# Selections, state-space products and gate products tied to the newest matmul, and engine orders from a time-line model

## The chip, the cores and the metric

The kernel runs on one core of one Trainium2 chip, as one launch. The metric is the device time in microseconds (us), the median of several runs. A core has a matrix engine (TensorE, PE in the profile; its weight loads are PEld), VectorE (DVE), ScalarE (ACT), GpSimd (POOL) and SyncE (SP), each with an instruction queue of its own that is worked off in order, and queues of DMA transfers that SP, ACT and POOL start. Matmuls write into PSUM, of which the kernel uses eight banks by turns; everything else lies in SBUF.

## What is computed

Two transformer-like blocks over 512 tokens of width 1024, all in float32. The first is a feed-forward layer, attention of several kinds (compressed, selected, windowed) and a second feed-forward layer. The second is a gated linear recurrence beside a state-space layer (the mix), and then a layer of 16384 small experts (PEER). The parts that the change touches, cut:

```python
def _s5(u, a_re, a_im, log_dt, b_re, b_im, c_re, c_im, d_skip, w_glu, b_glu):
    ...
    bb_re = coef_re * br - coef_im * bi
    bb_im = coef_re * bi + coef_im * br
    ...
    _, _, xr, xi = lax.associative_scan(combine, (a_re_t, a_im_t, bu_re, bu_im), axis=1)
    ...

def _peer(h, w_q, keys1, keys2, u_tab, v_tab):
    ...
    def block(hb):
        qh = (hb @ w_q).reshape(tb, PEER_HEADS, 2, PEER_HALF)
        s1 = jnp.einsum('thd,nd->thn', qh[:, :, 0], keys1)
        s2 = jnp.einsum('thd,nd->thn', qh[:, :, 1], keys2)
        v1, i1 = lax.top_k(s1, PEER_TOPK)
        v2, i2 = lax.top_k(s2, PEER_TOPK)
        cand = (v1[..., :, None] + v2[..., None, :]).reshape(tb, PEER_HEADS, kk)
        cidx = (i1[..., :, None] * PEER_NKEYS + i2[..., None, :]).reshape(tb, PEER_HEADS, kk)
        best, pos = lax.top_k(cand, PEER_TOPK)
        eidx = jnp.take_along_axis(cidx, pos, axis=-1)
        gates = jax.nn.softmax(best.astype(jnp.float32), axis=-1).astype(hb.dtype)
        act = jax.nn.gelu(jnp.einsum('td,thkd->thk', hb, u_tab[eidx]), approximate=False)
        return jnp.einsum('thk,thkd->td', gates * act, v_tab[eidx])
```

## The kernel before

**Products.** A large product is written as three matmuls on split operands (`mm3`: high and low part of the weights and of the input), 512 columns each. `weight` loads a 128 x 1024 block by SP (`raw`), casts it on ScalarE (`whi`, L173) and subtracts on VectorE, in one stage on GpSimd, to get the low part (`wlo`, L174); it does so two blocks ahead of their use. A product of one such block is 24 matmuls.

**Order of the program.** `weave` writes the program. A main generator gives the large products; side generators give the rest. `self.clk` adds up a rough time of all matmuls written so far (model time, in ns), and a side that yields 8000 goes on when 8000 of it have passed. So every side instruction has a place among the matmuls. That place is not binding: when the program is complete, the framework lays out the queue of each engine by running the instructions through a model of the machine. There an instruction may go ahead of those written before it on its engine once all that it depends on is done, so one that depends on nothing late can be laid out long before its place. Then waits between engines are set by the data and buffers alone.

**Preparation of the state space** (`s5_prepare`): a side of the second feed-forward stage. For each of four quarters it makes two groups of six elementwise instructions of 512 or 576 columns on GpSimd, by the helpers `mul`, `sub` and `add` (L1015 to L1021), then transposes, stores to HBM and some VectorE work.

**Routing of the experts** (`peer_route`): while the products of the experts run, VectorE finds the sixteen best candidates per token and head. `select(t, gap)` turns them, for 128 tokens (tile t of 4), into numbers of experts and gates: a subtraction on GpSimd (L1522), Exp on ScalarE (L1523), and twice a conversion (L1538, L1539), sixteen comparisons `eq` (L1548) and two sums `sel` (L1553) on VectorE; four transposes bring the result into `routeT` and `routeG`. `dense(t)` then makes a dense table of gates out of it: for each token a one-hot matrix `a` (GpSimd, L1569) and `b` (VectorE, L1570), one matmul (`b,a`), and two instructions that put the result into `stage` (ScalarE L1594, VectorE L1595), which goes to HBM. The one-hots are made two groups of four tokens ahead. `select(0)` is written ahead of `dense(0)`, `select(t + 1)` beside `dense(t)`, in thirteen steps of 8000 of model time.

**Experts' second half** (`peer`, `load`): for each of 128 blocks of experts the activations come back from HBM (`t`), are multiplied by the gates on GpSimd (L1687) and split on ScalarE (`pwh`, L590) and VectorE (`pwl`, L591). Sixteen groups of eight blocks; each group's are loaded while the group before is multiplied.

Of the kernel before, what the change touches and what calls it, by code (L numbers as in the profile page):

```python
# [13 lines left out]
ALU = mybir.AluOpType  # L14
AX = mybir.AxisListType
# [7 lines left out]
FT = 22  # L23
GB = 16
AHEAD = 2


class Weights:
# [21 lines left out]
class Prog:  # L50
# [23 lines left out]
    def mm(self, out, lhsT, rhs, start, stop):  # L74
        n = m = 1
        for x in rhs.shape[1:]:
            n *= x
        for x in lhsT.shape[1:]:
            m *= x
        p = 4 if lhsT.dtype == F32 else 1  # L80
        self.clk += max(n * 0.4217 * p, m * 0.84 * (2 if p == 4 else 1))
        self.nc.tensor.matmul(out, lhsT=lhsT, rhs=rhs, start=start, stop=stop)  # L82

    def tr(self, out, x, ident):
        self.clk += 54
# [132 lines left out]
    def small(self, n, w=4):  # L218
        t = self.big.tile([128, 64], F32, tag="rs_small", bufs=3, name=self.name("rs"))
        return [t[:, w * i:w * i + w] for i in range(n)]  # L220
# [791 lines left out]
        return pn  # L1012

    def mul(self, eng, out, a, b):
        eng.tensor_tensor(out, a, b, op=ALU.mult)  # L1015

    def sub(self, eng, out, a, b):
        eng.tensor_tensor(out, a, b, op=ALU.subtract)

    def add(self, eng, out, a, b):  # L1020
        eng.tensor_tensor(out, a, b, op=ALU.add)  # L1021

    def mix_consts(self):
        nc, A, ph = self.nc, self.A, self.ph
# [13 lines left out]
    def s5_prepare(self):  # L1038
        nc, A, ph = self.nc, self.A, self.ph
# [87 lines left out]
        for j in range(4):  # L1127
# [4 lines left out]
            pr, pi = (pd[:, i, :, q].rearrange("p l g -> p g l")[:, :, :, None].to_broadcast(sh) for i in range(2))  # L1132
            br, bi = (bb[:, i, q, :][:, :, None, :].to_broadcast(sh) for i in range(2))
            t, R = self.t2k(), [self.t2k(), self.t2k()]
            self.mul(g, f4(R[0]), pr, br)
            self.mul(g, f4(t), pi, bi)
            self.sub(g, R[0], R[0], t)
            self.mul(g, f4(R[1]), pr, bi)
            self.mul(g, f4(t), pi, br)
            self.add(g, R[1], R[1], t)  # L1140
            yield 13000
            for i in range(2):
                ps = self.ps()
                for a in range(4):
# [8 lines left out]
            cr, ci = (m["s5c"][:, i, q, :][:, :, None, :].to_broadcast(sh) for i in range(2))  # L1153
            ca = [ph.tile(sh, F32, tag="ca", bufs=3, name=self.name("ca")) for _ in range(3)]
            flat = lambda t: t.rearrange("p g l h -> p (g l h)")
            self.mul(g, ca[0], pr, cr)
            self.mul(g, ca[2], pi, ci)
            self.sub(g, flat(ca[0]), flat(ca[0]), flat(ca[2]))
            self.mul(g, ca[1], pnb, cr)
            self.mul(g, ca[2], pr, ci)  # L1160
            self.sub(g, flat(ca[1]), flat(ca[1]), flat(ca[2]))
            yield 15000
            for i in range(2):
                g.dma_start(second[:, 1024 + 576 * i:1600 + 576 * i], flat(ca[i]))
            ps = self.ps()
# [304 lines left out]
    def peer_route(self, st, box):  # L1470
# [46 lines left out]
        TG = ph.tile([128, 512, 2], F32, name="routeG")  # L1517

        def select(t, gap):
            gate = small(128, F32, "gate", 2)  # L1520
            gv = gate.rearrange("p (h k) -> p h k", h=8)
            g.tensor_tensor(gv, best[:, t], best[:, t, :, 0:1].to_broadcast([128, 8, 16]), op=ALU.subtract)  # L1522
            nc.scalar.activation(gate, gate, AF.Exp)  # L1523
            sm = small(8, F32, "gsum", 2)
            v.tensor_reduce(sm, gv, axis=AX.X, op=ALU.add)
            v.reciprocal(sm, sm)
            v.tensor_tensor(gv, gv, sm[:, :, None].to_broadcast([128, 8, 16]), op=ALU.mult)
            gh = small(128, F32R, "gateh", 2)
            gl = small(128, F32, "gatel", 2)
            v.tensor_copy(gh, gate)  # L1530
            v.tensor_tensor(gl, gate, gh.bitcast(F32), op=ALU.subtract)
            yield gap
            sel = []
            p2 = pos[:, t].rearrange("p h k -> p (h k)")
            for i, (op, c) in enumerate(((ALU.logical_shift_right, 4), (ALU.bitwise_and, 15))):
                ji = small(128, U32, "ji", 2)
                jf = small(128, F32, "jf", 2)
                v.tensor_scalar(ji, p2, c, None, op0=op)  # L1538
                v.tensor_copy(jf, ji)  # L1539
                o = small(128, F32, "sel", 4)  # L1540
                xf = ph.tile([128, 8, 16], F32, tag="idxf", bufs=2, name=self.name("xf"))
                v.tensor_copy(xf, idx[i][:, t])
                eq = ph.tile([128, 128, 16], F32, tag="eq", bufs=1, name=self.name("eq"))

                ev = eq.rearrange("p (h k) j -> p h k j", h=8)
                jv = jf.rearrange("p (h k) -> p h k", h=8)
                for j in range(16):
                    v.scalar_tensor_tensor(ev[:, :, :, j], jv, float(j), xf[:, :, j:j + 1].to_broadcast([128, 8, 16]),  # L1548
                                           op0=ALU.is_equal, op1=ALU.mult)
                    if j % 4 == 3:  # L1550
                        yield gap
                for s in (slice(0, 64), slice(64, 128)):
                    v.tensor_reduce(o[:, s], eq[:, s], axis=AX.X, op=ALU.add)  # L1553
                    yield gap
                sel.append(o)
            ps = self.ps()
            for i, x in enumerate(sel + [gh.bitcast(F32), gl]):
                self.tr(ps[:, i * 128:(i + 1) * 128], x, self.ident)
            ts = slice(t * 128, (t + 1) * 128)
            for i in range(2):  # L1560
                nc.scalar.copy(T2[i][:, ts], ps[:, i * 128:(i + 1) * 128])
            nc.scalar.copy(TG[:, ts, :].rearrange("p t x -> p x t"), ps[:, 256:512].rearrange("p (x t) -> p x t", x=2))
# [12 lines left out]
        def dense(tile):  # L1575
            t1 = tile * 128
            ab = [onehots(t1), onehots(t1 + 4)]
            yield 5500
            due = self.clk
            for t0 in range(0, 128, 4):  # L1580
                if t0 % GB == 0:
                    stage = ph.tile([128, 128, GB], F32, tag="stage", bufs=3, name=self.name("stage"))
                a, b = ab.pop(0)
                pss = [self.ps(), self.ps()]
                for i in range(4):
                    self.mm(pss[i // 2][:, (i % 2) * 256:(i % 2) * 256 + 256], lhsT=a[:, i, :],
                            rhs=b[:, i].rearrange("p x e -> p (x e)"), start=True, stop=True)
                if t0 + 8 < 128:
                    ab.append(onehots(t1 + t0 + 8))
                for i in range(2):  # L1590
                    o = t0 % GB + 2 * i
                    sv = stage[:, :, o:o + 2].rearrange("p e t -> p t e")
                    pv = pss[i].rearrange("p (t x e) -> p t x e", t=2, x=2)
                    nc.scalar.copy(sv, pv[:, :, 0])  # L1594
                    v.tensor_tensor(sv, sv, pv[:, :, 1], op=ALU.add)  # L1595
                if t0 % GB == GB - 4:
                    nc.scalar.dma_start(self.gd[(t1 + t0) // GB], stage)
                due = max(due + self.pace, self.clk - 3000)
                yield max(0, due - self.clk)
# [29 lines left out]
    def peer(self, st, done):  # L1629
# [53 lines left out]
        def load(e):  # L1683
            t = self.t2k()
            nc.scalar.dma_start(t, gs[e])
            yield 3600
            g.tensor_tensor(f(t), f(t), gts[e // 8][:, :, e % 8, :], op=ALU.mult)  # L1687
            yield 2600
            hi = self.ph.tile([128, 512], F32R, tag="pwh", bufs=16, name=self.name("pwh"))
            lo = self.ph.tile([128, 512], F32R, tag="pwl", bufs=16, name=self.name("pwl"))  # L1690
# [249 lines left out]
```

## Time and profile before

| what | us |
|---|---|
| median of three runs | 3064.87 |
| lowest and highest | 3063.09, 3072.38 |
| the profiled execution | 3067.61 |
| its span, first to last instruction | 3065.8 |
| TensorE busy in it | 3001.5 (98%) |
| VectorE, ScalarE, GpSimd busy | 2052.5, 1167.6, 1068.7 |

The stages follow one another: first feed-forward to about 405 us, attention to 760, second feed-forward to 1190, mix to 1475, candidates for the experts to 1715, dense gates to 2284, the second half of the experts to the end. TensorE is close to full everywhere, so the profile is read by its gaps: who released it, and what that engine did before. A row of a time line gives start and duration in us, the engine and line, what it writes and reads, how many equal instructions follow each other (x8), and in brackets the idle time of its engine before it, with the releaser.

### The profile page before, as it was taken

The page shows a single profiled execution, that of the slowest core. Times are in us where ns is not written, and L with a number is a line of the kernel's source. Part 1 is how long each engine was busy: PE and PEld are TensorE (multiplying, and loading weights), DVE is VectorE, ACT ScalarE, POOL GpSimd, SP SyncE. Part 2 cuts the span into 40 slices and gives each one's busy share as a digit, 9 for nine tenths or more (in the row PEclk, how much of TensorE's full clock was granted, in tenths as well). Part 3 has the DMA queues.
Part 4 walks back from the last instruction along what each step waited for, and adds up shares of the span by engine and source line. Part 5 has one row for each costly group of instructions (what it writes and reads, how often), then busy time and mean ns, then how long its engine had stood idle before and what let it go on. Part 6 is the DMA issues. An engine that isn't in the chain of part 4 may idle for free.

```text
span 3065.8 us, 40068 instructions
## 1 busy us (share of the span) xinstructions
PE 3001.5 (98%) x14672; PEld 2470.7 (81%) x14672; DVE 2052.5 (67%) x3902; ACT 1167.6 (38%) x1851; POOL 1068.7 (35%) x1016
## 2 busy tenths in 40 slices
PE   8999999999999999899999899999999999999998
PEld 6888886667887889787888788888887888888887
DVE  7455457775768656874778998878863655665653
ACT  4222334453422236444433354545443322332232
POOL 1000110002344422012345787878752423322321
PEclk9999999999999999999999999999999999999999
DMA  6344322113535443222333355555557656656642
GB/s 200 105 146 137 96 87 83 49 39 95 169 116 182 158 135 118 77 71 83 99 111 120 130 194 191 189 188 192 183 197 248 219 189 208 192 183 194 201 138 76
DMA packets 140324, 443.54 MB, mean 145 GB/s; under 512 B 16720, under 2 KB 19568, under 8 KB 135008
## 3 DMA queue, kind: packets, MB, share of 16 engines
q1 hardware_dynamic: 82512, 285.41, 29.4%
q10 hardware_dynamic: 42624, 101.73, 9.1%
q0 software_dynamic: 14992, 53.85, 5.6%
q8 instruction: 116, 1.90, 0.3%
q14 instruction: 80, 0.66, 0.1%
HBM read 361.88 MB, written 77.86 MB: 143 GB/s over the span
## 4 chain that ended last, share of the span: by engine, by line
PE 71%; DVE 5%; DMA 1%; issue 1%; ACT 1%; POOL 1%; DVEq 0%; ACTq 0%; POOLq 0%
PE ps L82 70%; DVE wlo L174 1%; DVE eq L1548 1%; DMA t<-act_d 1%; PE ps L86 1%; POOL t L823 0%; DVE sel L1553 0%; POOL t L1687 0%; ACT whi L173 0%; DMA act_d<-t 0%; DVE h L1817 0%; ACT t L966 0%; DVE jf L1539 0%; DVE t L821 0%; DVE t L591 0%
## 5 line engine op out<-in xcount | busy, mean ns | idle before, releaser
L173 ACT CAST whi<-raw 128x1024 fp32r<-128x1024 f32 (+2 forms) x505 | 516.7, 1025 | 1114.0 <-PE ps L82 886.9
L82 PE MATMUL ps<-xhi,whi 128*128 128x512 f32 (+1 forms) x2232 | 873.7, 392 | 12.3 <-ACT whi L173 10.8
L82 PE MATMUL ps<-xhi,wlo 128*128 128x512 f32 (+1 forms) x2232 | 862.1, 387 | 2.7 <-POOL wlo L174 1.8
L82 PE MATMUL ps<-xlo,whi 128*128 128x512 f32 (+1 forms) x2232 | 862.7, 387 | 0.8 <-DVE xlo L382 0.7
L174 DVE TENSOR_TENSOR wlo<-raw,whi 128x1024 fp32r<-128x1024 f32 (+2 forms) x469 | 603.6, 1287 | 136.7 <-ACT whi L173 126.1
L82 PEld LDWEIGHTS ps<-xhi,whi 128*128 128x128 f32 x2232 | 421.2, 189 | 105.3 <-issue 14.1
L1569 POOL TENSOR_SCALAR a<-iota,routeT 128x128 fp32r<-128x128 f32 x512 | 459.8, 914 | 108.0 <-PE ps L82 107.9
L82 PEld LDWEIGHTS ps<-xhi,wlo 128*128 128x128 f32 x2232 | 420.3, 189 | 91.3 <-POOL wlo L174 2.2
L82 PEld LDWEIGHTS ps<-xlo,whi 128*128 128x128 f32 x2232 | 420.7, 189 | 80.3 <-issue 2.5
L82 PE MATMUL ps<-pwh,whi 128*128 128x512 f32 (+1 forms) x1048 | 403.3, 385 | 1.5 <-ACT pwh L590 1.5
L82 PE MATMUL ps<-pwh,wlo 128*128 128x512 f32 (+1 forms) x1048 | 403.2, 385 | 1.1 <-DVE wlo L174 1.1
L82 PE MATMUL ps<-pwl,whi 128*128 128x512 f32 (+1 forms) x1048 | 403.4, 385 | 0.3 <-DVE pwl L591 0.2
L1687 POOL TENSOR_TENSOR t<-t,gt 128x512 f32<-128x512 f32 x128 | 199.2, 1576 | 421.1 <-DMA t<-act_d 367.0
L1570 DVE SCALAR_TENSOR_TENSOR b<-iota,routeT,routeG 128x256 fp32r<-128x256 f32 x512 | 232.2, 503 | 64.5 <-PE ps L82 64.5
L1823 DVE SCALAR_TENSOR_TENSOR h<-ps,mod,h 128x512 f32<-128x512 f32 (+1 forms) x131 | 96.4, 736 | 220.5 <-PE ps L82 220.5
L82 PEld LDWEIGHTS ps<-pwh,whi 128*128 128x128 f32 x1048 | 197.1, 188 | 41.0 <-ACT pwh L590 2.1
L82 PEld LDWEIGHTS ps<-pwh,wlo 128*128 128x128 f32 x1048 | 197.4, 188 | 40.5 <-DVE wlo L174 1.5
L82 PEld LDWEIGHTS ps<-pwl,whi 128*128 128x128 f32 x1048 | 197.3, 188 | 40.1 <-DVE pwl L591 1.0
L1594 ACT COPY stage<-ps 128x256 f32<-128x256 f32 x256 | 137.8, 643 | 162.0 <-PE ps L82 152.8
L591 DVE TENSOR_TENSOR pwl<-t,pwh 128x512 fp32r<-128x512 f32 x128 | 140.7, 1127 | 45.4 <-ACT pwh L590 40.8
L268 POOL TENSOR_TENSOR acc<-acc,sq 128x512 f32<-128x512 f32 x18 | 32.0, 1777 | 382.2 <-ACT sq L264 381.8
L1595 DVE TENSOR_TENSOR stage<-stage,ps 128x256 f32<-128x256 f32 x256 | 147.3, 623 | 2.3 <-ACT stage L1594 2.3
(406 smaller groups left out, 3818.8 us busy)
## 6 DMA issues: line engine op xcount, KB each, us to landing
raw<-pu SPq DMA_DIRECT2D x128, 512.0 KB, 3.6
raw<-pv SPq DMA_DIRECT2D x128, 512.0 KB, 3.5
act_d<-t ACTq DMA_DIRECT2D x128, 256.0 KB, 2.5
gates_d<-stage ACTq DMA_DIRECT2D x32, 1024.0 KB, 4.4
gt<-gates_d POOLq DMA_DIRECT2D x16, 2048.0 KB, 13.9
t<-act_d ACTq DMA_DIRECT2D x128, 256.0 KB, 3.6
aw<-ada_w SPq DMA_DIRECT2D x48, 512.0 KB, 4.5
raw<-g SPq DMA_DIRECT2D x44, 512.0 KB, 3.7
```

The source lines that it names most:

```text
L82: self.nc.tensor.matmul(out, lhsT=lhsT, rhs=rhs, start=start, stop=stop)
L86: self.nc.tensor.transpose(out, x, ident)
L173: nc.scalar.copy(hi[:, :n], raw[:, :n])
L174: (nc.gpsimd if self.pool_lo else nc.vector).tensor_tensor(lo[:, :n], raw[:, :n], hi[:, :n].bitcast(F32), op=ALU.subtract)
L268: nc.gpsimd.tensor_tensor(st["acc"], st["acc"], sq, op=ALU.add)
L591: self.nc.vector.tensor_tensor(lo, x, hi.bitcast(F32), op=ALU.subtract)
L1569: g.tensor_scalar(a[:, i, :], iota, T2[0][:, c], None, op0=ALU.is_equal)
L1570: v.scalar_tensor_tensor(b[:, i], iota[:, None, :].to_broadcast([128, 2, 128]), T2[1][:, c], TG[:, t + i, :, None].to_broadcast([128, 2, 1 ...
L1594: nc.scalar.copy(sv, pv[:, :, 0])
L1595: v.tensor_tensor(sv, sv, pv[:, :, 1], op=ALU.add)
L1687: g.tensor_tensor(f(t), f(t), gts[e // 8][:, :, e % 8, :], op=ALU.mult)
L1823: nc.vector.scalar_tensor_tensor(x, ps, P.mod[:, 40 + d:41 + d], x, op0=ALU.mult, op1=ALU.add)
```

## The change

A helper `paced` adds a dependency of an instruction on the matmul written last, so that it may not start before that matmul is done, neither in the framework's model nor on the chip. It is put on instructions of `select` for tiles 1 to 3 (the gate subtraction, conversions, comparisons and sums), on the 48 products of `s5_prepare`, which also get a yield of 2200 after each in place of one yield per group, and on the 128 gate products of `load`. The first dense group of tile 0 is put at 9000 instead of 5500 of model time after its one-hots. And the context gets `schedule_with_timeline_sim=True`: the framework lays out the queues with its time-line model of the machine in place of its default one, for the whole kernel. No arithmetic changes.

```diff
+PACE = mybir.DependencyInfo(mybir.DependencyClass.Sync, mybir.DependencyReason.DATA)
...
-        self.nc.tensor.matmul(out, lhsT=lhsT, rhs=rhs, start=start, stop=stop)
+        self.last_mm = self.nc.tensor.matmul(out, lhsT=lhsT, rhs=rhs, start=start, stop=stop).ins.name
+
+
+    def paced(self, x):
+        self.tc.add_manual_dep(x.ins, self.last_mm, PACE, reason="pace")
...
-            self.mul(g, f4(R[0]), pr, br)
-            self.mul(g, f4(t), pi, bi)
-            self.sub(g, R[0], R[0], t)
-            self.mul(g, f4(R[1]), pr, bi)
-            self.mul(g, f4(t), pi, br)
-            self.add(g, R[1], R[1], t)
-            yield 13000
+            for op, *x in ((self.mul, f4(R[0]), pr, br), (self.mul, f4(t), pi, bi), (self.sub, R[0], R[0], t),
+                           (self.mul, f4(R[1]), pr, bi), (self.mul, f4(t), pi, br), (self.add, R[1], R[1], t)):
+                self.paced(op(g, *x))
+                yield 2200
+            yield 2000
...
-            self.mul(g, ca[0], pr, cr)
-            self.mul(g, ca[2], pi, ci)
-            self.sub(g, flat(ca[0]), flat(ca[0]), flat(ca[2]))
-            self.mul(g, ca[1], pnb, cr)
-            self.mul(g, ca[2], pr, ci)
-            self.sub(g, flat(ca[1]), flat(ca[1]), flat(ca[2]))
-            yield 15000
+            f0, f1, f2 = (flat(x) for x in ca)
+            for op, *x in ((self.mul, ca[0], pr, cr), (self.mul, ca[2], pi, ci), (self.sub, f0, f0, f2),
+                           (self.mul, ca[1], pnb, cr), (self.mul, ca[2], pr, ci), (self.sub, f1, f1, f2)):
+                self.paced(op(g, *x))
+                yield 2200
+            yield 3000
...
         def select(t, gap):
+            paced = self.paced if t else lambda x: None
...
-            g.tensor_tensor(gv, best[:, t], best[:, t, :, 0:1].to_broadcast([128, 8, 16]), op=ALU.subtract)
+            paced(g.tensor_tensor(gv, best[:, t], best[:, t, :, 0:1].to_broadcast([128, 8, 16]), op=ALU.subtract))
...
-                v.tensor_scalar(ji, p2, c, None, op0=op)
+                paced(v.tensor_scalar(ji, p2, c, None, op0=op))
...
-                v.tensor_copy(xf, idx[i][:, t])
+                paced(v.tensor_copy(xf, idx[i][:, t]))
...
-                    v.scalar_tensor_tensor(ev[:, :, :, j], jv, float(j), xf[:, :, j:j + 1].to_broadcast([128, 8, 16]),
-                                           op0=ALU.is_equal, op1=ALU.mult)
+                    paced(v.scalar_tensor_tensor(ev[:, :, :, j], jv, float(j),
+                                                 xf[:, :, j:j + 1].to_broadcast([128, 8, 16]),
+                                                 op0=ALU.is_equal, op1=ALU.mult))
...
-                    v.tensor_reduce(o[:, s], eq[:, s], axis=AX.X, op=ALU.add)
+                    paced(v.tensor_reduce(o[:, s], eq[:, s], axis=AX.X, op=ALU.add))
...
             ab = [onehots(t1), onehots(t1 + 4)]
-            yield 5500
+            yield 5500 if tile else 9000
...
-            g.tensor_tensor(f(t), f(t), gts[e // 8][:, :, e % 8, :], op=ALU.mult)
+            self.paced(g.tensor_tensor(f(t), f(t), gts[e // 8][:, :, e % 8, :], op=ALU.mult))
...
-    with tile.TileContext(nc) as tc:
+    with tile.TileContext(nc, schedule_with_timeline_sim=True) as tc:
```

## Rows read from the trace of the kernel before

**Rows 1.** The page's head and its engine line: busy us, share of span, instructions

```profile
span 3065.8 us, 40068 instructions
PE 3001.5 (98%) x14672; PEld 2470.7 (81%) x14672; DVE 2052.5 (67%) x3902; ACT 1167.6 (38%) x1851; POOL 1068.7 (35%) x1016
```

**Rows 2.** Waits of TensorE, whole span: releaser, us in total, times, longest us

```profile
PE ps L82 <- ACT whi L173: 12.1, 4, 9.7
PE ps L82 <- DVE b L1570: 6.6, 1, 6.6
```

**Rows 3.** Stretches (attention, mix): length, then busy us of each engine, clock

```profile
400.00:765.00 365.00, 351.65 (x1810) 253.49 (x1809) 244.90 (x577) 161.09 (x431) 30.65 (x20) 1.00 0.22 69
...
1190.00:1480.00 290.00, 277.27 (x1830) 237.48 (x1829) 200.66 (x395) 136.70 (x205) 41.28 (x43) 0.97 0.25 83
```

**Rows 4.** Time line of VectorE ahead of tile 0's first one-hots

```profile
1690.41 3.90 DVE L1548 SCALAR_TENSOR_TENSOR eq<-jf,xf 128x128 f32<-128x128 f32 x16
...
1710.19 3.94 DVE L1548 SCALAR_TENSOR_TENSOR eq<-jf,xf 128x128 f32<-128x128 f32 x16
...
1717.78 3.25 DVE L1570 SCALAR_TENSOR_TENSOR b<-iota,routeT,routeG 128x256 fp32r<-128x256 f32 x8
```

**Rows 5.** Time line of ScalarE in the same stretch

```profile
1690.79 0.31 ACT L1523 ACTIVATE gate<-gate 128x128 f32<-128x128 f32 x1 [9.51 <-POOL gate L1522]
...
1692.90 1.04 ACT L173 CAST whi<-raw 128x1024 fp32r<-128x1024 f32 x1
```

**Rows 6.** Time line of TensorE in the same stretch

```profile
1693.99 0.50 PE L82 MATMUL ps<-xhi,whi 128*128 128x512 f32 x1 [1.11 <-ACT whi L173]
...
1696.48 0.80 PE L82 MATMUL ps<-xhi,wlo 128*128 128x512 f32 x1 [1.76 <-POOL wlo L174]
...
1699.55 0.39 PE L82 MATMUL ps<-xhi,whi 128*128 128x512 f32 x1
1699.78 0.39 PE L82 MATMUL ps<-xlo,whi 128*128 128x512 f32 x1
...
1718.40 1.74 PE L82 MATMUL ps<-b,a 128*128 128x256 f32 x4 [6.63 <-DVE b L1570]
...
1723.35 0.40 PE L82 MATMUL ps<-xhi,wlo 128*128 128x512 f32 x1
```

**Rows 7.** Time lines of VectorE and GpSimd in the second feed-forward stage

```profile
910.28 10.76 DVE L174 TENSOR_TENSOR wlo<-raw,whi 128x1024 fp32r<-128x1024 f32 x1
...
981.02 10.17 DVE L463 TENSOR_TENSOR t<-t,sg 128x512 f32<-128x512 f32 x1
...
910.48 2.18 POOL L1015 TENSOR_TENSOR t<-pd,bb 128x512 f32<-128x512 f32 x2
...
918.52 1.42 POOL L1018 TENSOR_TENSOR ca<-ca,ca 128x576 f32<-128x576 f32 x1
```

**Rows 8.** Time line of TensorE after these

```profile
921.09 0.50 PE L82 MATMUL ps<-xhi,wlo 128*128 128x512 f32 x1 [0.93 <-DVE wlo L174]
...
994.11 0.50 PE L82 MATMUL ps<-ahi,wlo 128*128 128x512 f32 x1 [2.59 <-DVE wlo L174]
```

**Rows 9.** Time lines at the start of the experts' second half

```profile
2383.98 6.05 POOL L1687 TENSOR_TENSOR t<-t,gt 128x512 f32<-128x512 f32 x4
...
2384.43 4.46 DVE L174 TENSOR_TENSOR wlo<-raw,whi 128x1024 fp32r<-128x1024 f32 x1 [0.82 <-ACT whi L173]
...
2388.94 0.50 PE L82 MATMUL ps<-pwh,wlo 128*128 128x512 f32 x1 [1.08 <-DVE wlo L174]
```

**Rows 10.** The dense stage by stretches, all engines; then L1548 alone, on VectorE

```profile
1718.00:1860.00 142.00, 141.60 (x672) 118.86 (x673) 135.84 (x282) 67.54 (x111) 122.04 (x128) 0.98 0.50 175
1860.00:2284.00 424.00, 424.00 (x2046) 356.64 (x2045) 346.56 (x636) 206.24 (x335) 329.82 (x372) 1.00 0.54 189
2284.00:2328.00 44.00, 44.00 (x196) 36.42 (x195) 10.96 (x10) 13.13 (x18) 3.47 (x2) 1.00 0.66 224
...
1655.00:1718.00 63.00, 27.21 (x80) 0.96 0.35 117
```

More of the change, by code (lines that the diff above doesn't have):

```diff
@@ L1014, in mul @@
     def mul(self, eng, out, a, b):
-        eng.tensor_tensor(out, a, b, op=ALU.mult)
+        return eng.tensor_tensor(out, a, b, op=ALU.mult)
     def sub(self, eng, out, a, b):
-        eng.tensor_tensor(out, a, b, op=ALU.subtract)
+        return eng.tensor_tensor(out, a, b, op=ALU.subtract)
     def add(self, eng, out, a, b):
-        eng.tensor_tensor(out, a, b, op=ALU.add)
+        return eng.tensor_tensor(out, a, b, op=ALU.add)
     def mix_consts(self):
```

## The prediction

> **What bounds the kernel now.** I read the page's engine line first: TensorE is busy 3001.5 us of a span of 3065.8 [rows 1]. What is left is 64.3 us in which it stands, so no order of the other engines can bring more than that, plus what the clock loses after a stop. The second view is the list of whom TensorE waits for [rows 2]: the largest single waits are 9.7 us at the start, for the first cast weight (`whi`, a load from HBM, which the change doesn't touch), and 6.6 us for the one-hots `b` of L1570. The rest is many small waits. The third view is the stages: from 400 to 765 us (attention) TensorE stands 365.00 - 351.65 = 13.35 us, from 1190 to 1480 us (state-space mix) 290.00 - 277.27 = 12.73 us [rows 3]. So I looked for stops with one cause that the diff names.
>
> **Selections.** `select(t)` of the expert routing is needed tile by tile, but nothing in it depends on the matmuls. In 1655 to 1718 us VectorE executes 80 of the 128 comparison steps `eq` [rows 10]; tile 0 needs 32. From 1690.41 on, when two halves of 16 (tile 0's) are through, there come three more halves of 16, with their sums, before the first `b` of tile 0 at 1717.78 [rows 4]. TensorE stands there 6.63 us before `b,a` at 1718.40 [rows 6]. Just before, ScalarE waits 9.51 us for a later selection's gate (L1522 on GpSimd, L1523 on ScalarE); a `whi` cast queued behind it starts only at 1692.90 [rows 5], and TensorE stands 1.11 and 1.76 us [rows 6]. Together 6.63 + 1.11 + 1.76 = 9.5 us. After each stop the granted clock falls to the lower level for a while: eight matmul starts from 1696.48 to 1699.55 take 3.07 us, where 8 x 0.23 (from 1699.55 to 1699.78) is 1.84: 1.2 us lost. Twelve starts from 1718.40 to 1723.35 take 4.95 us, against eight of 0.23 and four of half the columns at 0.115, 2.3: 2.65 us lost [rows 6]. This place costs 9.5 + 1.2 + 2.65 = 13.4 us.
> The change makes 41 instructions in each of selections 1 to 3 (1 on GpSimd; on VectorE 2 x (1 + 1 + 16 + 2)) wait for the newest matmul at their place in the program. They leave the stretch before 1718 and go under the dense work of the tile before theirs. What lies between 1690.41 and 1717.78 for later tiles is some 27 us of VectorE, much more than the 6.63 by which `b` is late. The 3500 more of model time ahead of tile 0's dense work (5500 to 9000) put its first `b,a` about 3.7 us later among the matmuls, at no cost: it changes which matmul comes first, not how many there are; the stores of the gate table move by as much, and after the dense work TensorE still has 44 us of expert products to run, 44.00 of 44 busy in 2284 to 2328 [rows 10]. Cover for the moved work: in 1860 to 2284 us, where hardly a selection is left, VectorE is busy 346.56 of 424 us, 77 us free; and from 1718 to 1860, with 48 `eq` in it and VectorE busy 135.84 of 142, TensorE still ran 141.60 of 142 [rows 10]. So I count all 13.4 us. Without that cover the moved 27 us would come back.
>
> **State-space products.** `s5_prepare` issues two groups of six two-input products on GpSimd for each quarter. Eight of these run back to back from 910.48 to 919.9 us, and a VectorE `wlo` that begins at 910.28 takes 10.76 us; at 981.02 a product `t` takes 10.17 us in the same way [rows 7]. TensorE then stands 0.93 and 2.59 us, its weights or inputs late [rows 8]. VectorE, then, doesn't get in between such GpSimd instructions while they follow each other.
> The Trainium skill (SBUF — State Buffer, section "SBUF: two separate sides") says of the port that the two engines share that it is an exclusive lock which whoever starts first holds for the whole instruction. By that a VectorE instruction would wait for one product, about 1.4 us, not for eight. The trace goes beyond it; if the rule alone held, spacing would give nothing here and the sum below would come out 3.5 us higher.
> In the change each of the 48 products waits for the newest matmul and is followed by 2200 of model time, so between two of 1.1 to 1.5 us there is a hole for VectorE. Gain 0.93 + 2.59 = 3.5 us. The preparation gets 4 x (2200 + 1200), some 14 us, longer; it has the whole second feed-forward stage, and nothing before the mix reads it: 0. Behind a waiting product on GpSimd stand the quarter's stores and the additions of squares, with no near reader.
>
> **Gate products.** The 128 products L1687 are on GpSimd too. Four back to back at 2383.98 stretch a `wlo` to 4.46 us, and TensorE stands 1.08 us [rows 9]. Tied to four different matmuls they don't come in one run: gain 1.1 us. Queued behind them are the next gate loads (L1679); the casts `pwh` on ScalarE wait for them, and `whi` behind those. A product can only come later than now, but it is issued about a group of eight weights ahead of its use: 0.
>
> **Cost of the new waits.** 123 + 48 + 128 = 299 instructions get one. On VectorE `b`, the additions to `stage` and `wlo` stand behind a waiting selection. How much hold TensorE bears shows in the rows above: a hold of 10.76 us cost it 0.93 us, one of 10.17 cost 2.59 [rows 7, 8]. The selections come in 3 x 13 = 39 steps. Lower bound 0 (a wait for a matmul that is already done; no gain beyond those counted, since the waits only delay), upper bound 39 x 0.93 = 36 us. I take 3 us, three such steps: nearer to zero, as a wait should last a fraction of a product of 24 matmuls (24 x 0.23 = 5.5 us), half of those holds.
>
> **The engines' orders.** The flag lays out every queue anew; the trace of before can't show the new order. What it can touch is the 13.35 + 12.73 = 26.1 us of small waits in attention and mix [rows 3]. Bounds: all of it gone (-26), or as much again (+26). I take a quarter, -6.5: the waits come in short chains between VectorE, ScalarE and TensorE, which no order can remove wholly, and a model of time lines can at least see when an engine is busy. The least certain term.
>
> **Sum.** -13.4 - 3.5 - 1.1 + 3 - 6.5 = -21.5 us. The profiled execution took 3067.6 us (its span, 3065.8, and 1.8 around it), 2.7 above the median of 3064.9; 3067.6 - 21.5 = 3046.1 there, and 3064.9 - 21.5 = 3043.4 for the median: **3043 us**, 0.7% faster. Its own range, with the orders' term between -13 and 0 and the waits between 0 and 10: 3034 to 3057.
>
> **Rivals.**
> (1) The new orders clear most of the small waits: three quarters of 26.1 us, and some 5 us of lower clock with them (the granted clock is 0.97 over 1190 to 1480 [rows 3]). 3064.9 - 18.0 - 19.6 - 5 = 3022. For: the waits in those stages are short. Against: attention and mix are narrow chains.
> (2) The named stops go, but the new orders put others in attention and mix in their place, half as much again as now, +13: 3064.9 - 18.0 + 13 = 3060, no change that a measurement tells. For: the yields of the program were set with the old order. Against: TensorE waits there for many different groups, so there is no single one to lose.
> (3) Slower. The place is the dense stage: a later selection reaches the head of VectorE's queue before its matmul is done and holds the `b` behind it. Price: 0.93 us for each of 39 steps, +36, with the orders' term at 0: 3064.9 - 18.0 + 36 = 3083. It decides from holds longer than what TensorE's look-ahead bears: 10.76 less the 0.93 that came through, about 10 us (10.17 less 2.59, about 7.5, at the other place) [rows 7, 8]. Against: VectorE has 82% of that stage's later part filled [rows 10], so it tends to run behind TensorE rather than ahead. For: `b` stands directly behind.
> (4) The change doesn't do what it says: the later selections are laid out before the `b` as now, or something else holds `b`. Then 3065.
>
> **How the numbers follow.** Chances: forecast 0.53, (1) 0.12, (2) 0.14, (3) 0.16, (4) 0.05. A measurement of this kernel tells about 0.3% (9 us) from no change, so faster means under 3055.7 and slower over 3074.1. Faster: nearly all of the forecast (0.50), (1), and a fifth of (2): 0.65. Slower: most of (3), 0.15. The same: 0.20. The range reaches into (1) and into (3) until about 2 in 10 is out: 3020 to 3078.
>
> **What would show it.** Right: no later `eq` between tile 0's last sum and its first `b`; no wait over 1 us for `b`, `whi` or `wlo` near 1690 to 1720; granted clock 1.00 there; no VectorE instruction of 10 us in 900 to 1000 us, and the products on GpSimd apart from each other; TensorE's idle time near 47 us instead of 64.3 (the sum without the 3.9 us of clock). The orders' term: idle time of 400 to 765 and 1190 to 1480, now 13.35 and 12.73. Wrong: idle TensorE in 1720 to 2284, where there is next to none now, with VectorE or ScalarE waiting for TensorE at L1538 to L1553 or L1523 (3); more idle time in attention or mix (2); the first matmul later than 9.7 us.

## The result: 24.6 us slower, and the profile after

The changed kernel takes 3090.64 us (median of four runs, 3087.83 to 3092.50); the kernel before took 3066.05 beside it. The ratio is 1.0076, 95% interval 1.0060 to 1.0092. The forecast was 3043 with a range of 3020 to 3078, so the sign was wrong and the time lies outside the range.

The first thing to read is the engine line of the changed kernel, against [rows 1].

```profile
span 3088.0 us, 40003 instructions
PE 3026.1 (98%) x14672; PEld 2481.7 (80%) x14672; DVE 2005.9 (65%) x3902; ACT 1169.9 (38%) x1851; POOL 1010.6 (33%) x1016
```

TensorE leaves the same 14672 records of matmuls. It stands 61.9 us instead of 64.3. What grew by 24.6 us is its busy time, 3001.5 to 3026.1. So no stop explains the loss by itself; the same matmuls take longer. Which ones is seen stage by stage. The bounds are starts of matmuls that both kernels have: the last `ahi` of the first feed-forward stage, the first and the last `ahi` of the second, the first `keys`, the first `pwh`. So the row of attention also holds the first products of the second feed-forward stage. Lengths are in us, of one execution each; the other columns are the experiments below.

| stage | before | changed | default model, new waits | time-line model alone | changed, pinned in attention | changed, pairs of values tied |
|---|---|---|---|---|---|---|
| first feed-forward | 383.1 | 386.8 | 381.1 | 386.3 | 387.5 | 387.0 |
| attention | 478.9 | **511.5** | 480.2 | 513.7 | 490.7 | 495.7 |
| second feed-forward | 319.2 | 318.8 | 315.2 | 314.9 | 318.8 | 320.3 |
| mix | 310.4 | 318.7 | 311.5 | 320.4 | 323.0 | 319.1 |
| `keys` to first `pwh` | 858.8 | 843.1 | 844.5 | 858.2 | 843.1 | 843.1 |
| rest | 709.5 | 703.7 | 705.7 | 705.0 | 703.6 | 703.6 |

The place that the selections were to clear gained 15.7 us (forecast 13.4). Attention lost 32.6 and the mix 8.3. The stretches of the changed kernel show the same (columns as in [rows 3]; attention, the row of attention by its own bounds, the seam before the mix, dense stage):

```profile
405.00:799.00 394.00, 375.45 (x1798) 262.16 (x1797) 246.25 (x574) 158.28 (x427) 28.85 (x19) 0.97 0.20 63
...
386.80:898.30 511.50, 492.25 (x2334) 359.30 (x2334) 322.14 (x729) 206.69 (x495) 54.49 (x45) 0.98 0.26 81
...
1190.00:1240.00 50.00, 42.53 (x293) 40.89 (x294) 23.82 (x65) 21.32 (x40) 16.73 (x20) 0.86 0.35 125
...
1765.00:2315.00 550.00, 550.00 (x2655) 462.72 (x2654) 488.90 (x954) 275.78 (x443) 399.43 (x491) 1.00 0.53 187
```

and the row of attention before:

```profile
383.10:862.00 478.90, 465.53 (x2334) 348.28 (x2333) 324.33 (x729) 208.59 (x496) 74.21 (x57) 1.00 0.28 88
```

In the row of attention TensorE stands 511.50 - 492.25 = 19.25 us, against 478.90 - 465.53 = 13.37 before, 5.9 more. The other 26.7 of 32.6 are busy time (the granted clock, 0.98 against 1.00, has a part in it). In 1765 to 2315 it never stands, at a granted clock of 1.00: no new wait holds it there.

The costliest groups, TensorE's alone and each shape apart, name the matmuls (operation, shapes, count, busy us and mean ns of one, then idle time before them). First the kernel before, 400 to 765 us:

```profile
L82 PE MATMUL ps<-t,nat 128*64 128x256 f32 x112 | 18.9, 405 | 0.9 <-ACT t L656 0.9
...
L82 PE MATMUL ps<-t,nat 128*64 128x512 f32 x52 | 14.1, 614 | 1.5 <-ACT t L656 1.5
...
L82 PE MATMUL ps<-t,t 64*128 64x256 f32 x80 | 10.0, 389 | 0.0
...
L82 PE MATMUL ps<-t,t 64*128 64x512 f32 x32 | 8.4, 613 | 0.0
...
L82 PE MATMUL ps<-t,vcc 31*64 31x512 f32 x16 | 4.3, 612 | 0.0
...
L82 PE MATMUL ps<-t,t 64*128 64x128 f32 x48 | 3.2, 280 | 0.0
```

and the changed kernel, 400 to 800 us:

```profile
L85 PE MATMUL ps<-t,nat 128*64 128x256 f32 x112 | 24.6, 403 | 1.0 <-ACT t L663 1.0
L85 PE MATMUL ps<-t,nat 128*64 128x512 f32 x52 | 19.4, 618 | 2.6 <-ACT t L663 2.6
L85 PE MATMUL ps<-t,t 64*128 64x256 f32 x80 | 13.1, 398 | 0.0
...
L85 PE MATMUL ps<-t,t 64*128 64x512 f32 x32 | 11.6, 628 | 0.0
...
L85 PE MATMUL ps<-t,vcc 31*64 31x512 f32 x16 | 7.5, 613 | 0.0
...
L85 PE MATMUL ps<-t,t 64*128 64x128 f32 x48 | 6.1, 365 | 0.0
```

But for the last row the means of one matmul agree within 3% (405 and 403, 614 and 618, 612 and 613 ns), yet the sums grow by 5.7, 5.3, 3.1, 3.2, 3.2 and 2.9 us, 23.4 together. Busy time counts overlapping matmuls once, so equal means and a larger sum say that fewer of them overlap. These are the matmuls that use half of the array: 64 rows (queries by keys, `t,t`) or 64 columns (probabilities by values, `t,nat` and `t,vcc`). The program writes them in pairs, one for each half. The time lines of TensorE show both cases. Before:

```profile
612.11 1.08 PE L82 MATMUL ps<-t,nat 128*64 128x512 f32 x4 [0.68 <-ACT t L656]
```

and in the changed kernel:

```profile
636.78 0.82 PE L93 MATMUL ps<-ident,t 128*128 128x128 f32 x6
637.53 1.07 PE L85 MATMUL ps<-t,nat 128*64 128x512 f32 x2
638.53 1.13 PE L85 MATMUL ps<-t,t 64*128 64x256 f32 x4
```

Four records (each of these matmuls leaves two) take 1.08 us when the two halves stand next to each other; two records alone take 1.07. Records of opposite halves start 7 ns apart (the median), so the second matmul of a pair is free. The time-line model put something else between the two halves, since the second one's operand is ready a little later (the experiment "One wait more" bears this out), and then each half pays in full. Of the 45 pairs of values, 44 stand together in TensorE's queue before, and 22 in the changed kernel.

That half-array matmuls overlap, and that matmuls keep their order, the Trainium skill states as well (TensorE: Matmul & The Clock Gate, section "Part 3: Packing small matmuls — row/col tiling"): matmuls in different row groups run side by side with starts some 4 ns apart, and they start and end in the order of the queue. The trace agrees on the overlap, with 7 ns between starts for halves by rows as for halves by columns; no run here tests the order.

A low sum alone doesn't tell of sharing. The transposes `ident,t` use the whole array, and their sum too is well under count times mean (changed kernel, 400 to 800 us; 216 x 292 ns are 63 us):

```profile
L93 PE MATMUL ps<-ident,t 128*128 128x128 f32 x216 | 36.5, 292 | 9.8 <-DVE t L983 5.3 <-DVE t L941 3.8 <-ACT t L930 0.6
```

Records of whole-array matmuls that follow each other overlap as well (0.39 us long, 0.23 apart, at 1699.55 in [rows 6]). So a group's sum also depends on its neighbours' records, and TensorE's whole busy time is the check beside it: +24.6 us here.

### The profile page after: what moved, and what is told of

It is laid out like the page before. It is cut to its first block, busy times and chain, and to the rows that moved or that the text cites. A ratio compares the mean times of both kernels' runs of the same rounds, so it can differ in the third digit from the quotient of the medians.

```text
span 3088.0 us, 40003 instructions
## 1 busy us (share of the span) xinstructions
PE 3026.1 (98%) x14672; PEld 2481.7 (80%) x14672; DVE 2005.9 (65%) x3902; ACT 1169.9 (38%) x1851; POOL 1010.6 (33%) x1016
## 4 chain that ended last, share of the span: by engine, by line
PE 57%; DVE 2%; ACT 0%; issue 0%; POOL 0%; DVEq 0%; ACTq 0%
PE ps L85 56%; DVE wlo L181 0%; DVE t L1025 0%; DVE h L340 0%; DVE h L1823 0%; PE ps L93 0%; DVE t L1330 0%; DVE t L598 0%; POOL t L1022 0%; ACT whi L180 0%; DVE t L1313 0%; DVE t L1312 0%; DVE t L1460 0%; ACT t L597 0%; DVE sq L387 0%
## 5 line engine op out<-in xcount | busy, mean ns | idle before, releaser
L1575 POOL TENSOR_SCALAR a<-iota,routeT 128x128 fp32r<-128x128 f32 x512 | 416.7, 829 | 142.3 <-PE ps L85 142.1
L1693 POOL TENSOR_TENSOR t<-t,gt 128x512 f32<-128x512 f32 x128 | 183.5, 1439 | 462.2 <-PE ps L85 430.0
L85 PE MATMUL ps<-ahi,whi 128*128 128x512 f32 (+1 forms) x376 | 141.8, 379 | 0.0
```

What stands on the lines that cost most here:

```text
L85: self.last_mm = self.nc.tensor.matmul(out, lhsT=lhsT, rhs=rhs, start=start, stop=stop).ins.name
L1575: g.tensor_scalar(a[:, i, :], iota, T2[0][:, c], None, op0=ALU.is_equal)
L1693: self.paced(g.tensor_tensor(f(t), f(t), gts[e // 8][:, :, e % 8, :], op=ALU.mult))
```

## The experiments

Theory T: the loss is TensorE's order, by the pairs that it splits. Rivals: the new waits and yields cost; or operands really come later and the order doesn't matter.

**The time-line model alone.** The kernel before with one line changed.

```diff
-    with tile.TileContext(nc) as tc:
+    with tile.TileContext(nc, schedule_with_timeline_sim=True) as tc:
```

> The kernel before with the time-line model alone, no new waits and no new yields. Theory T (the order of TensorE's queue is what costs): the half-array matmuls of attention lose their neighbours as in the changed kernel, so attention is 479 + about 30 = 505 to 515 us long, start and mix are 10 us longer, and the stops at the selections and at the state-space products stay or move a little: 3095 to 3115 us. Rival P (the new waits and longer yields cost, the order is harmless): 3055 to 3075 us, attention 475 to 485.

Measured: 3104.29 us, ratio 1.0105 (1.0088 to 1.0121). Attention takes 513.7 us and 22 pairs of values stand together, as in the changed kernel. The loss needs no new wait. The stop at the one-hots is there, and longer (11.1 us for `b`, against 6.6 in [rows 2]).

**The new waits alone.** The changed kernel with the default model.

```diff
-    with tile.TileContext(nc, schedule_with_timeline_sim=True) as tc:
+    with tile.TileContext(nc) as tc:
```

> The changed kernel with the default model: all new waits and yields, without the time-line model. Theory T: the stops at the selections (-13.4), products (-3.5) and gate products (-1.1) go and attention keeps its 479 us: 3066 - 18 = 3048 us, range 3042 to 3060, the upper part if the longer preparation of the state space leaves a stop at the end of the second feed-forward stage. Rival P: at least 3085 us, with attention or the mix longer than before.

Measured: 3045.35 us, ratio 0.9921 (0.9909 to 0.9934): faster than both kernels. Its engine line:

```profile
span 3043.6 us, 40111 instructions
PE 2993.5 (98%) x14672; PEld 2465.6 (81%) x14672; DVE 2000.3 (66%) x3902; ACT 1173.0 (39%) x1851; POOL 1045.9 (34%) x1016
```

and its stretch around tile 0's first one-hots (columns as in [rows 3]), without a stop where [rows 6] has 6.63 us:

```profile
1700.00:1720.00 20.00, 20.00 (x96) 16.79 (x95) 18.60 (x46) 10.66 (x15) 17.76 (x23) 1.00 0.38 135
```

TensorE's busy time is 2993.5 us, 32.6 less than in the changed kernel. The rival on the waits falls. The signs that the prediction named for its edits are there: 32 of the 128 `eq` stand ahead of the first `b` instead of 80, GpSimd's products come in runs of at most four where before three runs are of eight and one of ten, and no VectorE instruction of the second feed-forward stage takes more than 5.12 us.

**TensorE's order pinned in attention.** The changed kernel; from the start of attention's weaving to its end every matmul and transpose is kept behind the one written before it. It is an order of issue, not a wait.

```diff
...
+        x = self.nc.tensor.matmul(out, lhsT=lhsT, rhs=rhs, start=start, stop=stop)
+        self.last_mm = x.ins.name
+        if self.pin:
+            self.tc.keep_in_program_order(x)
...
```

> The changed kernel, but TensorE's instructions of attention stand in its queue in the order in which the program writes them; the other engines keep the time-line model's order, and so does TensorE elsewhere. Theory T: the pairs of half-array matmuls stand next to each other again, their rows lose 20 to 23 us of busy time, and with some of the clock attention comes to 480 to 490 us: 3060 to 3073 us. Rival W (the changed kernel's attention is long because TensorE's operands come later, whatever the order): the pairs share their time again, but TensorE waits for them instead: attention 500 us or more, 3082 to 3095 us.

Measured: 3071.37 us, ratio 1.0003 (0.9995 to 1.0012). Attention falls from 511.5 to 490.7, 20.8 us back (0.7 above what was expected of it). The pairs (groups of TensorE, 400 to 780 us):

```profile
L85 PE MATMUL ps<-t,nat 128*64 128x256 f32 x112 | 18.3, 405 | 0.7 <-ACT t L670 0.7
L85 PE MATMUL ps<-t,nat 128*64 128x512 f32 x52 | 14.9, 616 | 2.5 <-ACT t L670 2.4
...
L85 PE MATMUL ps<-t,t 64*128 64x256 f32 x80 | 10.6, 392 | 0.0
...
L85 PE MATMUL ps<-t,t 64*128 64x512 f32 x32 | 9.0, 612 | 0.8 <-ACT t L937 0.8
...
L85 PE MATMUL ps<-t,vcc 31*64 31x512 f32 x16 | 4.3, 612 | 0.0
...
L85 PE MATMUL ps<-t,t 64*128 64x128 f32 x48 | 3.2, 280 | 0.0
```

and the same stretch as a whole (columns as in [rows 3]):

```profile
400.00:780.00 380.00, 360.88 (x1825) 261.06 (x1824) 255.32 (x581) 162.83 (x434) 29.72 (x19) 0.98 0.21 66
```

TensorE's idle time there, 380.00 - 360.88 = 19.1 us, stays where the changed kernel had it (18.55). All that came back is busy time, as T has it.

**The pairs split on purpose.** The kernel before; a yield between the two halves, the sum of yields unchanged.

```diff
...
             for i in range(2):
+                box["got"][i] += 1
...
+                if i == 0:
+                    yield 900
...
-            yield 1800
+            yield 900
```

> The kernel before with the default model, in which the two matmuls of each pair that multiplies probabilities with values stand 900 ns of model time apart (the same number of yields in sum, the same matmuls), so that other matmuls come between them. Theory T: each of the 112 of 256 columns costs about 309 ns instead of a mean of 151, each of the 52 of 512 columns 520 instead of 258, each of the 16 for the compressed branch 518 instead of 251: 17.8 + 13.5 + 4.3, about +35 us at most, +20 to +38 us with what stays next to another pair's half: 3086 to 3104 us. Rival (their place among the others doesn't matter, the pairs were not sharing time): within 5 us of 3066.

Measured: 3105.30 us, ratio 1.0122 (1.0105 to 1.0139), +37 us. The groups of TensorE, 397 to 803 us:

```profile
L82 PE MATMUL ps<-t,nat 128*64 128x256 f32 x112 | 33.0, 403 | 0.0
L82 PE MATMUL ps<-t,nat 128*64 128x512 f32 x52 | 27.1, 662 | 8.2 <-ACT t L656 8.2
...
L82 PE MATMUL ps<-t,vcc 31*64 31x512 f32 x16 | 8.5, 613 | 0.0
```

The three rows take 68.6 us instead of 37.3: 31.3 of the 37 are the price of the lost neighbour. TensorE's whole busy time agrees, 3038.3 us against 3001.5, 36.8 more. The time is 1.3 us above the range expected. The rival that they shared no time falls.

**One wait more.** The pin also changes all the rest of attention's order. So the pairs of values alone: in the changed kernel, the first matmul of a pair waits for the second's operand too.

```diff
...
+                if i == 0:
+                    self.tc.add_manual_dep(x.ins, t[2], PACE, reason="pair")
```

> The changed kernel with one more wait: of each pair of matmuls that multiplies probabilities with values, the first waits for the second's operand too, so that the model sees both ready at once and lays them next to each other; TensorE's order is otherwise free. Theory T (a pair that is split costs twice): the rows of values (256 and 512 columns, and the compressed branch) go back by 5.4 + 4.7 + 3.0 = 13.1 us of busy time, attention from 511.5 to 496 to 500 us, 3074 to 3081 us in all, although nothing was made ready earlier. Rival V (the pinned order gained for another reason, and a wait more can only delay): 3086 us or more, attention 507 or more.

Measured: 3073.73 us, ratio 1.0019 (1.0011 to 1.0028), 17 us less than the changed kernel, by a wait that was added. All 45 pairs of values stand together again. The groups of TensorE, 400 to 785 us:

```profile
L85 PE MATMUL ps<-t,nat 128*64 128x256 f32 x112 | 17.8, 402 | 0.4 <-DVE t L665 0.3
L85 PE MATMUL ps<-t,nat 128*64 128x512 f32 x52 | 14.0, 617 | 4.9 <-ACT t L665 3.8 <-DVE t L665 1.2
...
L85 PE MATMUL ps<-t,vcc 31*64 31x512 f32 x16 | 4.3, 612 | 0.0
```

36.1 us instead of 51.5, and attention 15.8 shorter; TensorE's whole busy time is 3007.6 us, 18.5 less than in the changed kernel. Idle time before the 512-column rows grew by 2.3 us (2.6 to 4.9), part of the price of the wait. The rival falls: that split pairs cost, and what the pairs of values cost here, is shown. For the pairs of queries by keys only the pin speaks: their three rows go from 30.8 back to 22.8 us under it, but no run tied them alone. And with the values tied attention is still 16.8 us above the 478.9 of before.

**All of TensorE pinned**, in the changed kernel and in the kernel before: the pin above, in every stage.

```diff
-        self.nc.tensor.matmul(out, lhsT=lhsT, rhs=rhs, start=start, stop=stop)
+        self.tc.keep_in_program_order(self.nc.tensor.matmul(out, lhsT=lhsT, rhs=rhs, start=start, stop=stop))
```

> The changed kernel with all of TensorE's instructions in the order in which the program writes them, in all stages; the other engines keep the time-line model's order. Theory T2 (what the changed kernel loses outside attention, 10 us in start and mix, is also due to TensorE's own order): start 383, mix 310 to 313 us, 3055 to 3063 us. Rival O (there it is the order of the other engines, by which TensorE's operands come later): mix stays at 318 to 323 us and start at 386: 3065 to 3075 us.

> The kernel before (default model, no new waits) with TensorE's instructions in the order in which the program writes them. With the same order of TensorE under the time-line model the mix took 331 us and attention 491. Theory O (there the other engines' orders cost, the program's order of TensorE is harmless): attention 478 to 484, mix 309 to 314 us, 3060 to 3072 us. Rival Q (the program's order of TensorE is itself poor, outside attention above all): mix 322 us or more, 3078 us or more.

Measured: 3090.60 us, ratio 1.0082 (1.0069 to 1.0095), and 3101.57, ratio 1.0117 (1.0101 to 1.0132). Attention takes 491.1 and 490.5 us, the mix 331.2 and 333.3, whichever model orders the other engines. My theory failed in both, and in the first its rival too; Rival Q of the second holds: the order in which the program writes TensorE's work is itself poor, by 12 us in attention (478.9 before) and 23 in the mix (310.4). It follows that the 12 us by which the pinned attention above stays behind the kernel before are the pin's own price, and hint at nothing in the other engines. For the mix, this pin can't tell TensorE's order from that of the others.

**The state-space products under the time-line model.** The changed kernel with the code of before for the products:

```diff
...
-                self.paced(op(g, *x))
-                yield 2200
-            yield 2000
...
+            yield 13000
...
```

> The changed kernel with the state-space products as before (no waits, old yields), all else as changed. Theory S (under the time-line model the paced products push the fourth quarter's end on GpSimd ahead of the sums of squares at the end of the second feed-forward stage): the stops of 3.5 and 2.7 us there go, that stage is 315 us long and the mix some 4 us shorter: 3081 to 3086 us. Rival (the stops come from the orders alone): 3088 to 3095 us.

Measured: 3083.21 us, ratio 1.0052 (1.0039 to 1.0065), 7 us less than the changed kernel by the medians (its interval, 1.0060 to 1.0092, touches this one, so the size is uncertain; the stages show 4.2 in the second feed-forward stage). GpSimd's time line in the changed kernel, at the seam to the mix:

```profile
1163.82 2.44 POOL L1025 TENSOR_TENSOR ca<-ca,ca 128x576 f32<-128x576 f32 x1 [1.57 <-PE ps L85]
...
1174.27 8.49 POOL L1182 DMA_DIRECT2D t<-t  x16 [6.14 <-issue]
1182.77 2.55 POOL L309 TENSOR_TENSOR acc<-acc,sq 128x512 f32<-128x512 f32 x2
```

and TensorE's:

```profile
1208.49 0.61 PE L85 MATMUL ps<-ones,acc 128*128 128x1 f32 x4 [3.54 <-POOL acc L309]
...
1220.01 1.22 PE L85 MATMUL ps<-ident,rs 128*128 128x128 f32 x4 [2.67 <-DVE rs L333]
```

The last quarter's products end late, and its 16 DMA issues stand ahead of the sums of squares. With the old code both stops are gone and the second feed-forward stage takes 314.6 us, as expected. So the edit of the products makes these stops; the way from the issues at 1174.27 to a sum that is late 25 us after them is not shown, as GpSimd idles in between, 4.31 and 5.32 us, for ScalarE's squares. The old code needs no wait here: under the time-line model no VectorE instruction of the stage takes more than 5.32 us. The mix didn't get shorter (320.3 us), so that half of the expectation failed.

**Three kernels with the default model** sort out the named stops. The first dense group at 9000, alone:

```diff
-            yield 5500
+            yield 5500 if tile else 9000
```

> The kernel before with one thing alone: the first dense group of tile 0 at 9000 instead of 5500 of model time. Theory T (the later tiles' selections stand ahead of tile 0's one-hots, whatever the place of the first dense matmul): the first matmul of the dense table comes later among the others by at most 3.5 us, so the stop of 6.63 us falls to about 3 at best and the two stops before it (1.11, 1.76) stay: 0 to -4 us, 3063 to 3069 us. Rival D (the selections are harmless, the matmul just came too early): the stop goes and the clock loss with it, -9 us or more, at most 3059 us.

Measured: 3067.02 us, ratio 1.0006 (0.9997 to 1.0015). From `keys` to the first `pwh` 854.6 us, 4.2 less. TensorE's time line keeps the first two stops of [rows 6] and has a smaller third:

```profile
1696.43 0.50 PE L82 MATMUL ps<-xhi,whi 128*128 128x512 f32 x1 [1.11 <-ACT whi L173]
...
1698.92 0.66 PE L82 MATMUL ps<-xhi,wlo 128*128 128x512 f32 x1 [1.76 <-POOL wlo L174]
...
1718.91 1.74 PE L82 MATMUL ps<-b,a 128*128 128x256 f32 x4 [1.76 <-DVE b L1570]
```

The later selections' waits alone (in `select` as in the change, 5500 kept):

```diff
+            paced = self.paced if t else lambda x: None
...
+                paced(v.tensor_copy(xf, idx[i][:, t]))
...
+                    paced(v.tensor_reduce(o[:, s], eq[:, s], axis=AX.X, op=ALU.add))
```

> The kernel before with the waits in the later selections alone; the first dense group stays at 5500 of model time. Theory T (the later tiles' work ahead of the first one-hots is the whole of that place's loss): the three stages from the first product with the keys to the first block of the experts' second half take 858.8 - 13.4 = 845.4 us, 3050 to 3056 us in all. Rival D2 (both are needed, the place of the first dense group gave 4 us alone): 849 us or more in these stages, 3057 us or more in all.

Measured: 3051.01 us, ratio 0.9959 (0.9946 to 0.9973). From `keys` to the first `pwh` 844.6 us, 14.2 less, and no stop from `keys` to the last `b,a`. So the waits in the selections are the whole of it, and the 9000 adds nothing beside them: the kernel with both has 844.5.

The state-space products spaced in the program, without their waits (the lines are those of the change):

```diff
-                self.paced(op(g, *x))
+                op(g, *x)
```

> The kernel before with the state-space products written 2200 of model time apart, as in the changed kernel, but without their wait for a matmul. Theory T (a place in the program binds nothing, the wait does): the products still come in runs on GpSimd, VectorE instructions of 10 us stay in 900 to 1000 us, and the second feed-forward stage keeps its length of 319 us: 3064 to 3071 us. Rival Y (the spacing in the program is enough): the products come singly, that stage is 315 us long as in the kernel with the new waits and the default model: 3061 to 3065 us.

Measured: 3060.05 us, ratio 0.9979 (0.9967 to 0.9991). Neither side is borne out. The stage gets shorter, against my theory; but GpSimd's queue still has the products in runs, against the rival, and VectorE is still held:

```profile
917.71 8.13 DVE L463 TENSOR_TENSOR t<-t,sg 128x512 f32<-128x512 f32 x1
...
998.82 7.06 DVE L174 TENSOR_TENSOR wlo<-raw,whi 128x1024 fp32r<-128x1024 f32 x1 [0.21 <-ACT whi L173]
```

Yet TensorE doesn't stand in that stage, which takes 314.1 us. Holds of 7 to 8 us cost nothing where those of 10.76 and 10.17 in [rows 7] cost 0.93 and 2.59. The last kernel is the whole change with the default model and, by the same edit, without these waits:

> All of the change but two things: the default model stays, and the state-space products get the yields without the waits. Theory Y (the waits of these products add nothing to the spacing): the second feed-forward stage 314 us instead of 315.2, mix 310 instead of 311.5, 3041 to 3045 us. Rival: the waits are needed beside the other edits, and a stop at these products is back: 3046 to 3050 us.

Measured: 3044.17 us, ratio 0.9933 (0.9919 to 0.9946), the same as with the waits (0.9909 to 0.9934). The second feed-forward stage takes 315.5 us and the mix 310.9. In the time these waits are worth nothing that can be measured. The trace has what the rival named all the same: two runs of eight products are back, VectorE is held longer than in any row above, and TensorE stands 1.13 us.

```profile
1077.10 12.08 DVE L598 TENSOR_TENSOR alo<-t,ahi 128x512 fp32r<-128x512 f32 x1
...
1090.97 0.50 PE L85 MATMUL ps<-xhi,wlo 128*128 128x512 f32 x1 [1.13 <-DVE wlo L181]
```

## Why the prediction was wrong, point by point

- **Selections: right.** Forecast 13.4 us, measured 14.2 alone and 15.7 in the changed kernel. The 2.65 of clock after the stop show too: the dense stage, first to last `b,a`, went from 565.2 to 562.5 us without any stop in either. The 1.2 of clock after the earlier stop was misread: from 1696.48 to 1699.55 seven matmuls start and not eight, so 7 x 0.23 = 1.6 and 1.5 us were lost, 13.7 for the place. That 9000 in place of 5500 is worth nothing beside them was right.
- **State-space products: gain right, reason half wrong.** Forecast 3.5, measured 4.0 with the default model. But other positions of the same runs give 5.1 without a wait, and the time-line model gives 4.3 (314.9) with nothing done to the products. "Nothing before the mix reads it: 0" failed under the time-line model: behind the last quarter stood the sums of squares, which I had written off as having no near reader, and they stopped TensorE for 3.54 and then 2.67 us.
- **Gate products.** Forecast 1.1. The last stage lost 3.8 us with the default model and 4.5 with the time-line model alone, which has no such wait; this can't be put down to the edit.
- **New waits: smaller than forecast.** I took 3 us; in 1765 to 2315 TensorE stands 0. Rival (3), the dense stage, is refuted. What they cost is at the seam, under the time-line model.
- **The engines' orders: the step that failed.** I bounded the term by the idle time of attention and mix, -26 to +26, and took -6.5. The two models differ by 3090.64 - 3045.35 = 45 us beside the new waits, and by 1.05%, 32 us, without them. The mistake was to let an order touch only TensorE's waits: "no order of the other engines can bring more than that", the 64.3 us in which it stands. An order also sets what TensorE's busy time is, since the second half of a pair that stands together is free; the rows of such pairs grew by 23.4 us of attention's 32.6, and 5.9 are more idle time. It was to be seen before: four records of some 600 ns each in 1.08 us at 612.11. Rival (2), orders that put new stops in place of the old, has the direction of the term but not the mechanism.
- **The sum without that term** was 3064.9 - 18.0 + 3 = 3049.9. The kernel that has only these edits is at 0.9921, 3041 us of 3064.9 (3037 to 3045), 9 us less: the 3 us of waits that didn't come are part of it, and the rest can't be put down to one edit.

Open stays what the mix (8.3 us) and the first feed-forward stage (3.7) lose; in the latter the kernels with the default model differ by 2.3 us among themselves (380.8 to 383.1). The mix before and in the changed kernel:

```profile
1181.00:1492.00 311.00, 297.46 (x1974) 256.16 (x1974) 215.12 (x427) 151.29 (x226) 45.67 (x52) 0.97 0.27 89
...
1217.00:1536.00 319.00, 302.54 (x1982) 260.01 (x1982) 214.26 (x433) 152.81 (x228) 47.02 (x52) 0.96 0.26 86
```

There 2.9 us are idle time (13.5 to 16.5) and 5.1 busy time; no group of TensorE's grew by more than 1.6 us, so no one group explains it as the pairs do in attention. The pins couldn't separate it, and without the stops at the seam the mix was no shorter.

## What to carry to other kernels

Before anything that reorders a queue, look for half-array matmuls that share the array: several records in a time line that together take the time of one, as 612.11 against 637.53 above. Their order is worth time that no list of waits shows. A busy sum under count times mean is only a hint, as whole-array matmuls have it too; a sum that grows at an equal mean, with TensorE's whole busy time, is the sign that it was lost. Tie such a pair, for instance by letting its first half wait for the operand of the second; that wait gave back 17 us here. Try a new order of all engines apart from edits that have a stop with a name: here the edits gained 23 us with the default model, and the order took 45.

## What was unexpected of the hardware

Two half-array matmuls of 512 columns, next to each other, take 1.08 us together and 1.07 us each alone. And a VectorE instruction of 0.69 us stretched to 8.13 us beside GpSimd's products cost TensorE nothing, while one stretched to 10.17 was followed by a stop of 2.59, and one stretched to 12.08 by a stop of 1.13.
